# Strided attention on one core: jumps taken out, waits declared as implied, buffers fixed, key and value preparation merged, zeros written by VectorE

## The chip, the cores and the metric

The kernel runs on one core of a Trainium2 chip. The time is device time in microseconds (us), the median of several runs. In the profile the engines are PE (TensorE, with its weight loads as PEld), DVE (VectorE), ACT (ScalarE), POOL (GpSimd) and SP (SyncE, which here only issues transfers).

## The reference

Attention over 8 x 12 = 96 heads, 1024 queries of 64 numbers each, in which every query attends to the same 16 keys: positions 0, 64, 128 and so on.

```python
batch, heads, seq, dim = (8, 12, 1024, 64)      # stride = 64, all float32
scale = 1.0 / np.sqrt(dim)
for i in range(seq):
    attend_positions = np.arange(0, seq, stride)
    q = Q[:, :, i:i + 1, :]
    k = K[:, :, attend_positions, :]
    v = V[:, :, attend_positions, :]
    scores = np.einsum('bhqd,bhkd->bhqk', q, k) * scale
    weights = np.exp(scores - np.max(scores, axis=-1, keepdims=True))
    weights = weights / (np.sum(weights, axis=-1, keepdims=True) + 1e-10)
    result[:, :, i, :] = np.einsum('bhqk,bhkd->bhqd', weights, v)[:, :, 0, :]
```

Q is read whole and the result is written whole, 25.2 MB each; of K and V only one row in 64 is read, 0.4 MB each.

## The kernel before, in words

The 96 heads are worked on in 24 groups of four. The order of the work is written out by hand: every engine executes its instructions in the order in which the program names them, and semaphores hold an instruction until what it needs is there.

**Transfers.** SP issues all of them, in one queue: K, Q of group 0, V, Q of groups 1 to 9 (`load`, ten buffers `qn`), and then in turn the result of group g (`store`, eight buffers `out_sb`) and Q of group g+10, up to group 23; the last ten are stores alone. That makes 50 transfers; 48 of them move 1 MB. Loads of groups 0 and 1 move pieces of 8 KB, the later loads pieces of 32 KB, stores pieces of 8 KB, K and V rows of 256 bytes. Each transfer also waits for the one issued eight before it, whose semaphore it uses again. All 1 MB transfers are written with the helper at L34, so L34 is both loads and stores. K is L100, V is L103.

**Preparation.** POOL makes an identity matrix and from it `perm_v` (L128), a matrix that replicates rows of V. VectorE and POOL write zeros into `k_t` (L132 for the first 8 groups, L134 for the other 16) and VectorE into `w_all` (L133). VectorE works out a selector `s_sel` from an iota (L136, L137), and from it the ones beside V (L138) and `mask` (L139). `key_rows` casts a third of K (L149, ScalarE) and transposes it (L150, VectorE); `keys` spreads it over `k_t` in copies of 32 partitions (L160). `value_rows` replicates half of V by two matmuls (L171) and evacuates each (L175). The first third of K and the first half of V come ahead of the loop, the rest inside it, at groups 1 to 7 and 4.

**A group.** `cast` turns Q into bfloat16, one half on POOL (L191), one on ScalarE (L192); `transpose` turns it on VectorE (L196); `scores` is four matmuls (L203) and two exponentials (L214, ScalarE); `values` multiplies V by the mask (L182, POOL); `outputs` is eight matmuls in three portions (L228), the reciprocal of the sums (L236, VectorE) and the product: two portions on VectorE (L238), the third copied by ScalarE (L240) and scaled by POOL (L241). Work ahead is staggered: while group g is put out, scores are made for g+1, transpose and values for g+2, casts for g+3.

**Alignment.** L87 and L102 call `addr_align(128, max_nops=0)` on VectorE, POOL and SP. It lets the following instruction stand at a multiple of 128 in the engine's stream and reaches it by a jump.

Buffers `qn`, `out_sb` and `qb` come from pools that hand them out in turn, and the framework derives every wait from who read and wrote a buffer before.

Of the kernel before, what the change touches and what calls it, by code (L numbers as in the profile page):

```python
# [9 lines left out]

FP32 = mybir.dt.float32
BF16 = mybir.dt.bfloat16
I16 = mybir.dt.int16
I32 = mybir.dt.int32
AF = mybir.ActivationFunctionType
ALU = mybir.AluOpType
# [8 lines left out]
def _copy(nc, out: bass.AP, in_: bass.AP):  # L25

    sides = [
        mybir.BassSymbolicTensorAccessPattern(
            ap=side.ap, dtype=side.dtype, bass_ap=side,
            is_dma=True, for_custom_bir_dma=True,  # L30
        )
        for side in (in_, out)
    ]
    return nc.sync.add_instruction(  # L34
        mybir.InstDMACopy(
            name=nc.get_next_instruction_name(), engine=mybir.EngineType.SP,
            ins=sides[:1], outs=sides[1:], queue="qSPDynamicHW",
            mode="Copy",
        )
    )  # L40
# [9 lines left out]
def kernel(  # L50
# [22 lines left out]
    OBUFS = 8  # L73

    const = ctx.enter_context(tc.tile_pool(name="const", bufs=1))
    qn_pool = ctx.enter_context(tc.tile_pool(name="qn", bufs=QBUFS))
    out_pool = ctx.enter_context(tc.tile_pool(name="outsb", bufs=OBUFS))
    qb_pool = ctx.enter_context(tc.tile_pool(name="qb", bufs=2))
# [14 lines left out]
    qn = {}  # L93

    def load(g):
        qn[g] = qn_pool.tile([P, 32 * D], FP32, name="qn", tag="qn")
        n = P if g < 2 else 32
        _copy(nc, qn[g], _ap_with(Q, [[HG * SD // n, n], [1, HG * SD // n]], g * HG * SD))

    nc.sync.dma_start(k_raw, _ap_with(K, kv_src))  # L100
    load(0)
    nc.sync.addr_align(128, max_nops=0)  # L102
    nc.sync.dma_start(v_raw, _ap_with(V, kv_src))  # L103
    for g in range(1, QBUFS):
        load(g)


    identity = const.tile([P, P], BF16, name="identity")
    ahead4 = const.tile([P, 4], I16, name="ahead4")
    slot4 = const.tile([P, 4], I16, name="slot4")  # L110
# [8 lines left out]
    nc.gpsimd.iota(ahead4, pattern=[[-16, 4]], base=64, channel_multiplier=1)  # L119
# [6 lines left out]
    for c in range(2):  # L126
        for a in range(2):
# [4 lines left out]
    nc.vector.memset(k_t[:, 0:8], 0.0)  # L132
    nc.vector.memset(w_all, 0.0)  # L133
    nc.gpsimd.memset(k_t[:, 8:NG], 0.0)  # L134

    nc.vector.tensor_single_scalar(out=slot4, in_=ahead4, scalar=48, op=ALU.bitwise_and)  # L136
# [7 lines left out]
    v_rep = const.tile([P, NC, 2, D], BF16, name="v_rep")  # L144


    def key_rows(m):
        part = slice(4 * m, 4 * m + 4)
# [7 lines left out]
    def keys(m, c):  # L156
        for s in range(4):
            src, dst, col = 32 * (2 * c + s % 2), 32 * (2 * (s % 2) + s // 2), NK + 32 * s
            op = nc.vector.tensor_copy if m == 0 and s >= 2 else nc.scalar.copy
            op(  # L160
                k_t[dst : dst + 32, 8 * m + c : 8 * m + 8 : 2, :, col : col + NK],
                k_r[src : src + 32, 4 * m : 4 * m + 4].rearrange(
                    "p n (a k f) -> p a n f k", a=2, f=2
                )[:, s // 2],
            )


    def value_rows(n):
        for c in range(2):
            vp = psum_sc.tile([P, NC // 2, D], FP32, name="vp", tag="sc")  # L170
            nc.tensor.matmul(  # L171
                vp, lhsT=perm_v[:, c].rearrange("p a b e k -> p (a b e k)"),
                rhs=v_bf[:, 6 * n : 6 * n + 6], start=True, stop=True,
            )
            nc.vector.tensor_copy(out=v_rep[:, 6 * n : 6 * n + 6, c], in_=vp)  # L175

    qb, qt, wt, vb, rec, out_sb = {}, {}, {}, {}, {}, {}


    def values(g):  # L180
        vb[g] = v_bufs[g % 3]
        nc.gpsimd.tensor_tensor(  # L182
            out=vb[g][:, 0 : 4 * D].rearrange("p (s d) -> p s d", s=4), in0=mask,
            in1=v_rep[:, g // 2, g % 2].unsqueeze(1).to_broadcast([P, 4, D]),
            op=ALU.mult,
        )

    def cast(g):
        qb[g] = qb_pool.tile([P, 32 * D], BF16, name="qb", tag="qb")
        half = 16 * D  # L190
        nc.gpsimd.tensor_copy(out=qb[g][:, 0:half], in_=qn[g][:, 0:half])  # L191
        nc.scalar.copy(qb[g][:, half:], qn[g][:, half:])  # L192

    def transpose(g):
        qt[g] = qt_pool.tile([P, 32 * D], BF16, name="qt", tag="qt")
        nc.vector.transpose(qt[g].bitcast(I32), qb[g].bitcast(I32))  # L196

    def scores(g):
        sc = psum_sc.tile([P, 512], FP32, name="sc", tag="sc")
        q = qt[g]  # L200
        for e in range(2):
            for f in range(2):
                nc.tensor.matmul(  # L203
                    sc, lhsT=k_t[:, g, f, NK * (1 - e) : NK * (1 - e) + P],
                    rhs=_ap_with(
                        q, [q.ap[0], [D, 8], [16 * D, 2], [2, 32]],
                        extra_offset=8 * D * e + f,
                    ),
                    start=e + f == 0, stop=e + f == 2,
                )  # L210
        w = wt[g] = w_bufs[g % 3]
        for a in range(2):
            wa = w[64 * a : 64 * a + 64]
            nc.scalar.activation(  # L214
                out=_ap_with(wa, [wa.ap[0], [P, 8], [1, 2], [2, 32]], extra_offset=64 * a),
                in_=sc[64 * a : 64 * a + 64].rearrange("p (t x q) -> p t x q", t=8, x=2),
                func=AF.Exp, bias=0.0, scale=scale,
            )


    def outputs(g, c):
        if c == 0:
            out_sb[g] = out_pool.tile([P, 4, 8, D], FP32, name="out_sb", tag="out_sb")
# [12 lines left out]
        nc.vector.reciprocal(r, ps[:, 0:n, 4 * D : 4 * D + 4])  # L236
        if c < 2:
            nc.vector.tensor_tensor(out=to, in0=o, in1=by, op=ALU.mult)  # L238
        else:
            nc.scalar.copy(to, o)  # L240
            nc.gpsimd.tensor_tensor(out=to, in0=to, in1=by, op=ALU.mult)  # L241

    def store(g):
        o = out_sb[g]
        _copy(
            nc,
            _ap_with(out, [[16 * D, P], [2 * SD, 2], [1, 16 * D]], g * HG * SD),
            _ap_with(o, [o.ap[0], [1, 1], [1, 32 * D]]),
        )

    key_rows(0)
    keys(0, 0)
    cast(0)
    transpose(0)
    keys(0, 1)
# [19 lines left out]
    for g in range(NG):  # L275
        if g > 0:
            ahead(g)
        for c in range(3):
            outputs(g, c)
        if g == 0:  # L280
            ahead(g)
        if g in (1, 5):
            key_rows(g // 4 + 1)
        if g in (2, 3, 6, 7):
            keys(g // 4 + 1, g % 4 - 2)
        if g == 4:
            value_rows(1)
        store(g)
        if g + QBUFS < NG:
            load(g + QBUFS)  # L290
# [33 lines left out]
```

## Time and profile before

| | |
|---|---|
| time, median of 3 runs | 128.98 us (128.76 to 129.75) |
| the profiled execution, its own time | 128.94 us |
| its span, first to last instruction | 127.2 us |
| busy: VectorE, ScalarE, POOL, TensorE | 88.4, 86.0, 79.5, 64.3 us |
| moved by DMA | 51.20 MB, mean 403 GB/s |
| a store, from issue to landing (least, median, most) | 10.1, 13.5, 19.6 us |

A page of the profile gives busy time by engine, the span in 40 slices of 3.2 us (busy share in tenths; for DMA the mean of 16 engines, and GB/s), the DMA queues, the chain of waits followed back from the last instruction, and groups of instructions by line. The trace behind it also answers for any stretch of time (windows), lists instructions in order of time, and keeps a record of every DMA packet and of every landing, that is, of each of the 16 semaphore steps with which a transfer ends. In a timeline line the columns are start, duration, engine, line, operation, out<-in and, in brackets, idle time before and what ended it; SPq is SP's queue of issues. Times in the text are from the start of the span.

### The profile page before, as it was taken

The numbers are of one execution on the slowest core, as the hardware profiler recorded it, in microseconds if no ns is written. First come the engines' busy times: TensorE is split into PE (matmuls) and PEld (weight loads), VectorE is DVE, ScalarE is ACT, GpSimd is POOL, SyncE is SP. The second block draws the span as 40 slices with busy tenths as digits, with TensorE's granted clock in tenths as the row PEclk, the third lists the DMA queues.
The fourth block names the chain that finished last, engine by engine and source line by source line (L and its number), as shares of the span: only waits on it lengthen the run. The fifth ranks groups of instructions, "written<-read, shape, count | busy, mean of one in ns | idle before, by whom it ended". The sixth has DMA issues, their size and how long they took to land.

```text
span 127.2 us, 1226 instructions
## 1 busy us (share of the span) xinstructions
PE 64.3 (51%) x292; PEld 30.2 (24%) x292; DVE 88.4 (69%) x162; ACT 86.0 (68%) x120; POOL 79.5 (62%) x84
## 2 busy tenths in 40 slices
PE   0006548196757619662787636666463797430000
PEld 0002223042323304330333313233232343110000
DVE  4956592769698786877887889797988876760000
ACT  4151917957999986999958997979798765620000
POOL 6941818645855994595867896969889673454000
PEclk9999999755699995999657999999999558975555
DMA  2999999989998998998999989989999999999980
GB/s 67 374 329 474 464 412 423 464 381 394 451 451 381 459 464 343 487 433 376 500 387 405 497 353 438 461 374 451 428 402 451 397 433 420 425 433 417 428 350 26
DMA packets 7911, 51.20 MB, mean 403 GB/s; under 512 B 3872, under 2 KB 3872, under 8 KB 3872
## 3 DMA queue, kind: packets, MB, share of 16 engines
q1 hardware_dynamic: 7904, 51.12, 96.5%
q8 instruction: 2, 0.03, 0.1%
q14 instruction: 5, 0.04, 0.1%
HBM read 25.95 MB, written 25.17 MB: 402 GB/s over the span
## 4 chain that ended last, share of the span: by engine, by line
POOL 35%; issue 32%; DMA 15%; DVE 4%; PE 2%; ACT 1%; POOLq 1%; SPq 0%; DVEq 0%
POOL qb L191 14%; POOL out_sb L241 12%; POOL v_all L182 9%; DMA out_dram<-out_sb 9%; DMA qn<-in_Q_dram 5%; PE sc L203 1%; POOLq L319 1%; DVE out_sb L238 1%; DVE qt L196 1%; DVE v_rep L175 1%; ACT qb L192 1%; PE vp L171 1%; ACT out_sb L240 1%; DVE rec L236 0%; SPq L100 0%
## 5 line engine op out<-in xcount | busy, mean ns | idle before, releaser
L228 PE MATMUL o_ps<-v_all,w_all 128*128 128x260 bf16 x192 | 38.4, 320 | 37.1 <-DVE out_sb L238 32.8
L241 POOL TENSOR_TENSOR out_sb<-out_sb,rec 128x768 f32<-128x768 f32 x24 | 35.3, 1471 | 29.8 <-ACT out_sb L240 29.8
L238 DVE TENSOR_TENSOR out_sb<-o_ps,rec 128x768 f32<-128x768 f32 (+1 forms) x48 | 39.6, 825 | 1.7
L214 ACT ACTIVATE w_all<-sc 64x512 bf16<-64x512 f32 x48 | 35.2, 734 | 5.5 <-PE sc L203 4.9
L203 PE MATMUL sc<-qt,k_t 128*128 128x512 bf16 x96 | 32.0, 466 | 10.7 <-DVE qt L196 10.7
L196 DVE STREAM_TRANSPOSE qt<-qb 128x1024 int32<-128x1024 int32 x24 | 29.6, 1232 | 10.8 <-ACT qb L192 5.7
L228 PEld LDWEIGHTS <-w_all 128*128 128x128 bf16 x192 | 18.9, 109 | 60.3 <-DVE out_sb L238 41.2
L240 ACT COPY out_sb<-o_ps 128x768 f32<-128x768 f32 x24 | 19.2, 798 | 16.1 <-DVE rec L236 15.8
L191 POOL CAST qb<-qn 128x1024 bf16<-128x1024 f32 x24 | 24.9, 1036 | 4.7 <-DMA qn<-in_Q_dram 4.7
L192 ACT CAST qb<-qn 128x1024 bf16<-128x1024 f32 x24 | 25.0, 1045 | 0.7
L236 DVE RECIPROCAL rec<-o_ps 128x12 f32<-128x12 f32 (+1 forms) x72 | 15.1, 210 | 6.3 <-PE o_ps L228 5.8
L182 POOL TENSOR_TENSOR v_all<-mask,v_rep 128x256 bf16<-128x256 bf16 x24 | 16.0, 668 | 0.6 <-DVE v_rep L175 0.6
L203 PEld LDWEIGHTS <-k_t 128*128 128x128 bf16 x96 | 10.8, 113 | 21.6 <-ACT k_t L160 8.1
L160 ACT COPY k_t<-k_r 32x128 bf16<-32x128 bf16 x20 | 5.9, 295 | 2.1 <-DVE k_r L150 1.9
L134 POOL MEMSET k_t<- 128x4608 bf16 x1 | 3.9, 3938 | 0.0
L175 DVE CAST v_rep<-vp 128x384 bf16<-128x384 f32 x4 | 2.2, 542 | 1.9 <-PE vp L171 1.8
L149 ACT CAST k_bf<-k_raw 128x256 bf16<-128x256 f32 x3 | 1.2, 406 | 3.2 <-DMA k_raw<-in_K_dram 3.2
L150 DVE STREAM_TRANSPOSE k_r<-k_bf 128x128 int32<-128x128 int32 x3 | 0.9, 310 | 2.3 <-ACT k_bf L149 2.3
L136 DVE TENSOR_SCALAR slot<-ahead 128x4 int16<-128x4 int16 x1 | 2.5, 2482 | 0.0
L171 PE MATMUL vp<-v_bf,perm_v 128*128 128x384 bf16 x4 | 1.6, 412 | 1.1 <-DVE v_rep L175 0.6
L132 DVE MEMSET k_t<- 128x1152 uint32 x1 | 1.0, 1018 | 1.6 <-PEq L305 1.6
L149 ACT ACT_TABLE_LOAD x1 | 1.3, 1283 | 0.7 <-PEq L305 0.7
(15 smaller groups left out, 5.7 us busy)
## 6 DMA issues: line engine op xcount, KB each, us to landing
qn<-in_Q_dram SPq DMA_DIRECT2D x24, 1024.0 KB, 14.7
out_dram<-out_sb SPq DMA_DIRECT2D x24, 1024.0 KB, 13.5
k_raw<-in_K_dram SPq DMA_DIRECT2D x1, 384.0 KB, 4.5
v_raw<-in_V_dram SPq DMA_DIRECT2D x1, 384.0 KB, 7.4
```

The lines of the kernel that those rows point to most:

```text
L160: op(k_t[dst : dst + 32, 8 * m + c : 8 * m + 8 : 2, :, col : col + NK], k_r[src : src + 32, 4 * m : 4 * m + 4].rearrange("p n (a k f) -> p ...
L182: nc.gpsimd.tensor_tensor(out=vb[g][:, 0 : 4 * D].rearrange("p (s d) -> p s d", s=4), in0=mask, in1=v_rep[:, g // 2, g % 2].unsqueeze(1).t ...
L191: nc.gpsimd.tensor_copy(out=qb[g][:, 0:half], in_=qn[g][:, 0:half])
L192: nc.scalar.copy(qb[g][:, half:], qn[g][:, half:])
L196: nc.vector.transpose(qt[g].bitcast(I32), qb[g].bitcast(I32))
L203: nc.tensor.matmul(sc, lhsT=k_t[:, g, f, NK * (1 - e) : NK * (1 - e) + P], rhs=_ap_with(q, [q.ap[0], [D, 8], [16 * D, 2], [2, 32]], extra_ ...
L214: nc.scalar.activation(out=_ap_with(wa, [wa.ap[0], [P, 8], [1, 2], [2, 32]], extra_offset=64 * a), in_=sc[64 * a : 64 * a + 64].rearrange( ...
L228: nc.tensor.matmul(ps[:, i, 0 : 4 * D + 4], lhsT=wt[g][:, i0 + i], rhs=vb[g], start=True, stop=True,)
L236: nc.vector.reciprocal(r, ps[:, 0:n, 4 * D : 4 * D + 4])
L238: nc.vector.tensor_tensor(out=to, in0=o, in1=by, op=ALU.mult)
L240: nc.scalar.copy(to, o)
L241: nc.gpsimd.tensor_tensor(out=to, in0=to, in1=by, op=ALU.mult)
```

## The change

- The jumps (L87, L102) are gone.
- `qn`, `qb` and `out_sb` are fixed buffers, indexed by group. For pairs of instructions between which another wait already guarantees the order, `implied` tells the framework to make no wait. `transpose(g)` gets a wait for store g−10, so that VectorE has waited for an output buffer before ScalarE and POOL use it.
- All of `k_t` is zeroed by VectorE. The selector comes from the identity by a reduction; its two copies move from VectorE to POOL.
- K is prepared in two parts (4 and 8 of 12) in place of three; copies that VectorE made for the first part are POOL's. The cast of V moves from VectorE to POOL.
- `value_rows` puts both matmuls into one slot of `o_ps` and evacuates them with one instruction.

```diff
-    for engine in (nc.vector, nc.gpsimd):
-        engine.addr_align(128, max_nops=0)
...
+    qn_bufs = [const.tile([P, 32 * D], FP32, name=f"qn{i}") for i in range(QBUFS)]
+    qb_bufs = [const.tile([P, 32 * D], BF16, name=f"qb{i}") for i in range(2)]
+    out_bufs = [const.tile([P, 4, 8, D], FP32, name=f"out_sb{i}") for i in range(OBUFS)]
...
+    def implied(ins, earlier, why):
+        tc.declare_no_dep(ins.ins, earlier.ins, reason=why)
...
     def load(g):
-        qn[g] = qn_pool.tile([P, 32 * D], FP32, name="qn", tag="qn")
+        qn[g] = qn_bufs[g % QBUFS]
...
+        if g >= QBUFS:
+            for earlier in (loaded[g - QBUFS], *cast_by[g - QBUFS]):
+                implied(loaded[g], earlier, "the store before it has waited for both casts")
...
     load(0)
-    nc.sync.addr_align(128, max_nops=0)
     nc.sync.dma_start(v_raw, _ap_with(V, kv_src))
...
-    nc.vector.memset(k_t[:, 0:8], 0.0)
+    nc.vector.memset(k_t, 0.0)
     nc.vector.memset(w_all, 0.0)
-    nc.gpsimd.memset(k_t[:, 8:NG], 0.0)
-
-    nc.vector.tensor_single_scalar(out=slot4, in_=ahead4, scalar=48, op=ALU.bitwise_and)
-    nc.vector.tensor_single_scalar(out=s_sel, in_=slot4, scalar=0, op=ALU.is_equal)
-    nc.vector.tensor_copy(out=v_all[:, :, 4 * D :], in_=s_sel.unsqueeze(1).to_broadcast([P, 3, 4]))
-    nc.vector.tensor_copy(out=mask, in_=s_sel.unsqueeze(2).to_broadcast([P, 4, D]))
+
+    nc.vector.tensor_reduce(
+        out=s_sel, in_=identity.rearrange("p (h s k) -> p s h k", h=2, s=4),
+        op=ALU.max, axis=mybir.AxisListType.XY,
+    )
+    nc.gpsimd.tensor_copy(out=v_all[:, :, 4 * D :], in_=s_sel.unsqueeze(1).to_broadcast([P, 3, 4]))
+    nc.gpsimd.tensor_copy(out=mask, in_=s_sel.unsqueeze(2).to_broadcast([P, 4, D]))
...
+    def keys(part, c, s):
+        src, dst, col = 32 * (2 * c + s % 2), 32 * (2 * (s % 2) + s // 2), NK + 32 * s
+        op = nc.gpsimd.tensor_copy if part is first and s >= 2 else nc.scalar.copy
...
     def value_rows(n):
+        vp = psum_o.tile([P, 3, 512], FP32, name="o_ps", tag="o")
+        rows = vp[:, 0:2, 0 : NC // 2 * D].rearrange("p c (n d) -> p c n d", d=D)
         for c in range(2):
-            vp = psum_sc.tile([P, NC // 2, D], FP32, name="vp", tag="sc")
...
-            nc.vector.tensor_copy(out=v_rep[:, 6 * n : 6 * n + 6, c], in_=vp)
+        nc.vector.tensor_copy(
+            out=v_rep[:, 6 * n : 6 * n + 6].rearrange("p n c d -> p c n d"), in_=rows
+        )
...
     def transpose(g):
         qt[g] = qt_pool.tile([P, 32 * D], BF16, name="qt", tag="qt")
-        nc.vector.transpose(qt[g].bitcast(I32), qb[g].bitcast(I32))
+        turned = nc.vector.transpose(qt[g].bitcast(I32), qb[g].bitcast(I32))
+        if g - 2 >= OBUFS:
+            tc.add_manual_dep(
+                turned.ins, stored[g - 2 - OBUFS].ins.name,
+                mybir.DependencyInfo(mybir.DependencyClass.Sync, mybir.DependencyReason.ANTI),
+                reason="frees the output buffer that VectorE fills next",
+            )
...
-            nc.scalar.copy(to, o)
-            nc.gpsimd.tensor_tensor(out=to, in0=to, in1=by, op=ALU.mult)
+            copied = nc.scalar.copy(to, o)
+            scaled[g] = nc.gpsimd.tensor_tensor(out=to, in0=to, in1=by, op=ALU.mult)
+            for past in range(g - OBUFS, -1, -OBUFS):
+                for earlier in (stored[past], scaled[past]):
+                    implied(copied, earlier, "VectorE has waited for the store")
+                implied(scaled[g], stored[past], "VectorE has waited for the store")
...
-    nc.vector.tensor_copy(out=v_bf, in_=v_raw)
+    nc.gpsimd.tensor_copy(out=v_bf, in_=v_raw)
     value_rows(0)
...
-        if g in (1, 5):
-            key_rows(g // 4 + 1)
-        if g in (2, 3, 6, 7):
-            keys(g // 4 + 1, g % 4 - 2)
+        if g == 1:
+            key_rows(rest)
+        if 2 <= g < 6:
+            for i in range(2 * g - 4, 2 * g - 2):
+                keys(rest, i // 4, i % 4)
         if g == 4:
             value_rows(1)
```

The casts, the exponentials and the masked values get `implied` declarations of the same kind, against the same instruction two or three groups earlier. Lines named in the prediction are those of the kernel before, but L205, which is `transpose` in the changed kernel.

More of the change, by code (lines that the diff above doesn't have):

```diff
@@ L12 @@
 BF16 = mybir.dt.bfloat16
-I16 = mybir.dt.int16
 I32 = mybir.dt.int32
@@ L144, with key_rows @@
     v_rep = const.tile([P, NC, 2, D], BF16, name="v_rep")
-    def key_rows(m):
-        part = slice(4 * m, 4 * m + 4)
+    def key_rows(part):
         nc.scalar.copy(k_bf[:, part], k_raw[:, part])
@@ L153, in key_rows @@
         )
[L156 to L165, printed above, removed]
+    def keys(part, c, s):
+        src, dst, col = 32 * (2 * c + s % 2), 32 * (2 * (s % 2) + s // 2), NK + 32 * s
+        op = nc.gpsimd.tensor_copy if part is first and s >= 2 else nc.scalar.copy
+        op(
+            k_t[dst : dst + 32, 2 * part.start + c : 2 * part.stop : 2, :, col : col + NK],
+            k_r[src : src + 32, part].rearrange(
+                "p n (a k f) -> p a n f k", a=2, f=2
+            )[:, s // 2],
+        )
     def value_rows(n):
+        vp = psum_o.tile([P, 3, 512], FP32, name="o_ps", tag="o")
+        rows = vp[:, 0:2, 0 : NC // 2 * D].rearrange("p c (n d) -> p c n d", d=D)
         for c in range(2):
-            vp = psum_sc.tile([P, NC // 2, D], FP32, name="vp", tag="sc")
             nc.tensor.matmul(
-                vp, lhsT=perm_v[:, c].rearrange("p a b e k -> p (a b e k)"),
+                rows[:, c], lhsT=perm_v[:, c].rearrange("p a b e k -> p (a b e k)"),
                 rhs=v_bf[:, 6 * n : 6 * n + 6], start=True, stop=True,
             )
-            nc.vector.tensor_copy(out=v_rep[:, 6 * n : 6 * n + 6, c], in_=vp)
+        nc.vector.tensor_copy(
+            out=v_rep[:, 6 * n : 6 * n + 6].rearrange("p n c d -> p c n d"), in_=rows
+        )
     qb, qt, wt, vb, rec, out_sb = {}, {}, {}, {}, {}, {}
@@ L181, in values @@
         vb[g] = v_bufs[g % 3]
-        nc.gpsimd.tensor_tensor(
+        masked[g] = nc.gpsimd.tensor_tensor(
             out=vb[g][:, 0 : 4 * D].rearrange("p (s d) -> p s d", s=4), in0=mask,
@@ L186, in values @@
         )
+        if g >= 3:
+            implied(masked[g], masked[g - 3], "the matmuls between them")
     def cast(g):
-        qb[g] = qb_pool.tile([P, 32 * D], BF16, name="qb", tag="qb")
+        qb[g] = qb_bufs[g % 2]
         half = 16 * D
-        nc.gpsimd.tensor_copy(out=qb[g][:, 0:half], in_=qn[g][:, 0:half])
-        nc.scalar.copy(qb[g][:, half:], qn[g][:, half:])
+        cast_by[g] = (
+            nc.gpsimd.tensor_copy(out=qb[g][:, 0:half], in_=qn[g][:, 0:half]),
+            nc.scalar.copy(qb[g][:, half:], qn[g][:, half:]),
+        )
+        if g >= 2:
+            for h in range(2):
+                for e in range(2):
+                    implied(cast_by[g][h], cast_by[g - 2][e], "the transpose between them")
     def transpose(g):
         qt[g] = qt_pool.tile([P, 32 * D], BF16, name="qt", tag="qt")
-        nc.vector.transpose(qt[g].bitcast(I32), qb[g].bitcast(I32))
+        turned = nc.vector.transpose(qt[g].bitcast(I32), qb[g].bitcast(I32))
[4 more added lines that the diff above has]
+                reason="frees the output buffer that VectorE fills next",
+            )
     def scores(g):
@@ L211, in scores @@
         w = wt[g] = w_bufs[g % 3]
+        raised[g] = []
         for a in range(2):
             wa = w[64 * a : 64 * a + 64]
-            nc.scalar.activation(
+            raised[g].append(nc.scalar.activation(
                 out=_ap_with(wa, [wa.ap[0], [P, 8], [1, 2], [2, 32]], extra_offset=64 * a),
@@ L217, in scores @@
                 func=AF.Exp, bias=0.0, scale=scale,
-            )
+            ))
+            for earlier in raised.get(g - 3, ()):
+                implied(raised[g][a], earlier, "the matmuls between them")
     def outputs(g, c):
         if c == 0:
-            out_sb[g] = out_pool.tile([P, 4, 8, D], FP32, name="out_sb", tag="out_sb")
+            out_sb[g] = out_bufs[g % OBUFS]
             rec[g] = rec_pool.tile([P, 8, 4], FP32, name="rec", tag="rec")
@@ L239, in outputs @@
         else:
-            nc.scalar.copy(to, o)
-            nc.gpsimd.tensor_tensor(out=to, in0=to, in1=by, op=ALU.mult)
+            copied = nc.scalar.copy(to, o)
[4 more added lines that the diff above has]
+                implied(scaled[g], stored[past], "VectorE has waited for the store")
     def store(g):
         o = out_sb[g]
-        _copy(
+        stored[g] = _copy(
             nc,
@@ L249, in store @@
         )
-    key_rows(0)
-    keys(0, 0)
+    first, rest = slice(0, 4), slice(4, NC)
+    key_rows(first)
+    for s in range(4):
+        keys(first, 0, s)
     cast(0)
     transpose(0)
-    keys(0, 1)
+    for s in range(4):
+        keys(first, 1, s)
     scores(0)
     cast(1)
-    nc.vector.tensor_copy(out=v_bf, in_=v_raw)
+    nc.gpsimd.tensor_copy(out=v_bf, in_=v_raw)
     value_rows(0)
```

11 lines of the change are left out of this document (3 added, 8 removed).

## The prediction, on record before the changed kernel ran

> **What bounds the kernel now.** I read the slices of the page first (part 2), then its queues (part 3), then the table of windows, and only then the engines.
>
> ```profile
> DMA  2999999989998998998999989989999999999980
> GB/s 67 374 329 474 464 412 423 464 381 394 451 451 381 459 464 343 487 433 376 500 387 405 497 353 438 461 374 451 428 402 451 397 433 420 425 433 417 428 350 26
> q1 hardware_dynamic: 7904, 51.12, 96.5%
> q8 instruction: 2, 0.03, 0.1%
> q14 instruction: 5, 0.04, 0.1%
> ```
>
> No computing engine is over 69% busy, but the one data queue keeps the 16 DMA engines busy for 96.5% of the span. The digits fall only in the first slice and the last two. The windows say the same with less jitter (after the PE, PEld, DVE, ACT and POOL columns come granted clock, DMA share, GB/s):
>
> ```profile
> 12.00:28.00 16.00, 9.64 (x34) 3.98 (x33) 9.40 (x17) 10.54 (x14) 8.76 (x10) 0.87 1.00 428
> 52.00:80.00 28.00, 17.55 (x89) 8.81 (x90) 23.45 (x44) 24.69 (x34) 21.18 (x22) 0.88 1.00 425
> 114.00:122.00 8.00, 0.00 (x0) 0.00 (x0) 0.00 (x0) 0.24 (x1) 1.47 (x1) 0.50 1.02 427
> ```
>
> In the last window almost nothing computes any more and the rate is what it was at 52 us: the queue has a full backlog from start to finish. So the chain of waits, which gives POOL 35% of the span, misleads: it follows computation back, while what ends last is the queue.
>
> From the landing records (16 per transfer, one for each DMA engine) I take the time apart. The first packet starts at 2.07 us; the mean landing of the 50th transfer is 124.42, so 51.12 MB took 122.35 us; its slowest engine lands 1.73 us after that mean; the span closes 1.02 us later, at 127.17; 1.74 us lie outside the span. The sum is 128.94, the profiled execution's own time, 0.04 under the median of the runs shown (128.98).
>
> **How much cover computation has.** SP issues the transfers in program order:
>
> ```profile
> 2.47 0.39 SPq L103 DMA_DIRECT2D v_raw<-in_V_dram  x1
> 2.91 9.84 SPq L34 DMA_DIRECT2D qn<-in_Q_dram  x9
> 21.14 0.63 SPq L34 DMA_DIRECT2D out_dram<-out_sb  x1
> 28.77 0.59 SPq L34 DMA_DIRECT2D out_dram<-out_sb  x1
> ...
> 112.93 3.43 SPq L34 DMA_DIRECT2D out_dram<-out_sb  x2
> ```
>
> A transfer needs 1.34 us from issue to first packet (0.73 to 2.07, the first one). The queue stays full if each is issued that long before its predecessor lands. The twelfth transfer lands at 30.86 (mean), so the first store may be issued up to 29.5 and is issued at 21.14: 8.4 us of cover. The second store (28.77) follows load 10, which lands at 35.76: 5.6 us. The last is issued at 115.8, and its predecessor lands at 121.98: 4.9 us. These are the two thinnest places. At the end cover does not depend on how fast computation runs before: load 23 lands complete at 101.24, POOL casts it at 102.00, and the last store follows 13.8 us after that cast, while ten stores (2.46 us each) are still to be moved after load 23.
>
> **The change, part by part.**
>
> *Jumps gone (L87, L102).* SP's jump lies between the issue of Q0, which ends at 1.95, and of V at 2.47: about 0.5 us. VectorE starts at 1.61 where ScalarE starts at 0.73: up to 0.9 us. POOL waits 0.83 us before L119. V is issued 0.5 us sooner, but the records show all 16 engines on K and Q0 until V's first packets at 6.4: worth 0. K's issue, at 0.73, stands before SP's jump and stays.
>
> *Shorter streams.* The built programs fall from 211 to 186 instructions on VectorE, 167 to 121 on ScalarE, 140 to 109 on POOL, 102 to 91 on SP; TensorE keeps 615. Most are separate semaphore waits: 42 to 5 on ScalarE, 45 to 10 on POOL. One takes 21 ns (median on VectorE's queue) or 17 ns (SP's), so 0.8, 0.7, 0.3 and 0.2 us on ScalarE, POOL, VectorE and SP, all under the queue. Fewer instructions also mean fewer fetches. In the packet records q14 moves 8 KB at 2.04, 3.18, 6.88, 48.85 and 81.97 us, 0.31 to 0.62 us each, and q8 16 KB at 48.58 and 91.35, 1.05 us each. A fetch holds one of 16 engines: 7 together take 4.0 us, 0.25 us of the mean. The two on q8 fall where TensorE has gone through some 190 and 430 instructions, so I take them as TensorE's and unchanged. If the five go, the mean gains 1.92/16 = 0.1 us. The slowest engine may gain more. Its lag is already 1.05 us at the second transfer, while the next slowest has 0.72, and it grows to 1.73. A fetch of 0.62 us at 2.04 lies just there. If it was on that engine and goes, the lag falls by 0.33, to the next engine's. Bounds: the whole 1.73 gone, or, with streams that now start unaligned, four fetches of 0.31 more on the slowest engine, +1.2. I take −0.3, by the row it comes from.
>
> [...]
>
> *Zeros on VectorE alone.* L132 takes 1.018 us for 1152 words, so 3456 words take 3.05; w_all keeps 1.34. POOL loses the 3.94 us of L134:
>
> ```profile
> 1.61 1.02 DVE L132 MEMSET k_t<- 128x1152 uint32 x1 [1.61 <-PEq L305]
> 2.67 3.94 POOL L134 MEMSET k_t<- 128x4608 bf16 x1
> 4.15 2.48 DVE L136 TENSOR_SCALAR slot<-ahead 128x4 int16<-128x4 int16 x1
> ```
>
> The odd row is the third: 2.48 us for four elements, ending at 6.63 when POOL's memset ends at 6.61; the next row like it (L137) takes 0.17. That stall goes. The new reduction lies between 0.17 (L137) and 0.56 (L258, 768 elements); 0.3. VectorE starts between 0.73 and 1.61 and is through at 5.4 to 6.6; k_bf is ready at 5.61, so the key transpose starts at 5.7 to 6.6, not 7.15. Worth 0: the first scores still wait for Q0, which lands at 8.2.
>
> *Keys, selector and V cast on POOL.* Two small copies of the selector and four of 32x128 join POOL: each above 0.22 (VectorE) and below 0.67 (L182, 256 elements), I take 0.4. They fit before 8.25 and, the last two, between 9.3 and the first scores at 10.67. What gets later is V. POOL takes its cast behind that of Q1, which starts at 12.31 and takes 1.04; the cast is 768/1024 of that, 0.78, bounds 0.56 (L258) and 1.04. Ready at 14.1, two matmuls (0.5 each) to 15.1, one evacuation in place of two (0.54 to 1.08) to 16.2, transpose(1) behind it to 17.5, then the first values (0.67) are in. The first reciprocal comes at about 18, not 16.39: 1.6 us later, 2.1 by the upper bounds. The first two stores move to about 22.7 and 30.4; their covers of 8.4 and 5.6 us swallow it, and past that each us of delay is a us at the end.
>
> *Merged keys and values later.* On ScalarE 16 copies of 0.295 become 8 between 0.295 and 0.59: 0 to 2.4 us saved. VectorE's two key transposes of 0.31 become one of 0.31 to 0.62. value_rows now takes a slot of o_ps: TensorE waits for one evacuation more (0.96), once at group 0 and once at group 4. Covered.
>
> *The new wait (L205).* From group 10 on, transpose(g) waits for store(g−10). Behind it in VectorE's queue stand the reciprocals and products of group g−2, which in the kernel before waited for that same store about 2.4 us later. It is thinnest at g = 23: the trace has that transpose at 103.07 and store 13 complete at 98.83. It holds by 4.2 us; if computation gains more than that, it only gives the surplus back. Worth 0.
>
> **Sum:** 128.94 − 0.1 − 0.3 = 128.5, all of it in how the fetches lie on the DMA engines; everything else is under the queue. With half of the −0.1 kept (two q14 fetches may stay), 128.6.
>
> [...]
>
> **The rivals.** *Forecast: the queue decides, 128.6* (87%). In it lies the case that the fetches do not change at all, that shorter streams fetch as often: 128.9.
>
> *Faster, 127.1* (7%): the lag of the slowest engine comes from the fetches as a whole. For it: the landing spread widens in steps near 48, 82 and 91 us, where fetches lie. Against: 1.05 of the 1.73 is there from the second transfer on and the lag creeps between steps; TensorE's two fetches stay. It needs 1.3 of 1.73 us.
>
> *Slower, 131* (6%): the V path through POOL lets the queue run dry before the second store. It decides once that store is issued after 34.4 (35.76 − 1.34). A delay of 8 us, to 36.8, would cost 2.4 us: 128.6 + 2.4 = 131.0. For it: three POOL instructions now stand between Q1's landing and the first values. Against: 1.6 to 2.1 us worked out; even a V cast as long as the 3.94 us memset makes 4.8.
>
> **From these to the numbers.** The runs before spread from 128.76 to 129.75, so about 1% (1.3 us) is what a measurement of this kernel can tell from no change. Range 127.9 to 129.7: below, 0.7 us more of the lag; above, the four extra fetches on the slowest engine (128.6 + 1.2 = 129.8), nearly whole. Faster 0.07, within 1% 0.87, slower 0.06.
>
> **What would show it.** Right: q1 still 51.12 MB at 96 to 97%, 425 to 428 GB/s in the same windows, first store at 22 to 24 us, last store issued well before 120, fewer than five q14 pieces, lag 1.3 to 1.7 us. Busy time of ScalarE and POOL may fall by several us with no effect. Wrong: a DMA digit under 8 between slices 3 and 37, a store issued after its predecessor's landing, or a lag that changed by over 1 us.

## The result and the profile after

The changed kernel takes 129.58 us (median, 129.29 to 129.81) beside 128.96 us of the kernel before, measured together: ratio 1.0037, 95% interval 1.0023 to 1.0050, so 0.30 to 0.64 us slower. The profiled execution took 129.29 us, of which 127.2 us are its span; the kernel before had 128.94. The profile after is of the fastest of the 22 executions, 0.29 us under their median, so it shows 0.35 us of the loss where the medians show 0.62. The prediction, 128.6 us, was 0.3% under the kernel before. The time lies in the range given and within 1%, but on the other side of no change.

The page of the changed kernel, slices of its part 2 and queues of its part 3:

```profile
DMA  2999999898998989999999989999999899999991
GB/s 65 360 320 492 423 402 454 371 474 340 505 407 369 513 348 417 461 379 438 461 384 443 477 363 469 430 387 492 402 387 484 363 420 430 425 420 430 425 410 59
q1 hardware_dynamic: 7904, 51.12, 97.0%
q8 instruction: 2, 0.03, 0.1%
q14 instruction: 4, 0.03, 0.1%
```

The queue still moves the same 51.12 MB in the same 7904 packets and still fills the span. No digit of the DMA line between slices 3 and 37 is under 8. So the queue never ran dry, and yet the kernel is slower; that points to the transfers themselves. The table of windows says where (stretch and length, then PE, PEld, DVE, ACT, POOL busy, granted clock, DMA share, GB/s):

```profile
12.00:28.00 16.00, 8.71 (x30) 3.58 (x29) 8.80 (x14) 9.91 (x12) 8.77 (x10) 0.93 0.99 416
52.00:80.00 28.00, 18.43 (x94) 9.27 (x95) 23.66 (x45) 23.96 (x30) 22.97 (x23) 0.88 1.01 428
114.00:122.00 8.00, 0.00 (x0) 0.00 (x0) 0.00 (x0) 0.00 (x0) 0.94 (x1) 0.50 1.01 425
```

In the middle and at the end the rate is that of before (425 and 427 there). In the first window, in which only loads move, it is 416 in place of 428 GB/s at a DMA share of 0.99: of these three stretches, this one alone lost, 2.8%.

The landing records, taken apart in the way of the prediction (us; an interval is that between mean landings of successive transfers):

| | before | after |
|---|---|---|
| loads Q1 to Q9, one interval | 2.427 | 2.485 |
| 12th transfer (Q9), mean landing | 30.62 | 31.27 |
| transfers 13 to 40, one interval | 2.458 | 2.453 |
| last ten stores, one interval | 2.461 | 2.464 |
| 50th transfer, mean landing | 124.18 | 124.88 |
| its slowest engine, after that | 1.73 | 1.40 |
| from that landing to the end of the measured time | 3.03 | 3.02 |
| sum: the profiled execution | 128.94 | 129.29 |

The prediction and the recorded expectations count landings and packets from a zero that lies 0.24 us ahead of the span's start, which is the zero of the timeline and of this table. Their first packet at 2.07 us is at 1.83, as the profile's own window shows, which has data moving before 2.00 us:

```profile
0.00:2.00 2.00, 0.00 (x0) 0.00 (x0) 0.39 (x1) 1.27 (x1) 0.79 (x8) 1.00 0.04 10
```

Their 30.86 is 30.62 here, and their 2.79 us from the last landing to the end is 3.03. Intervals, lags and differences between kernels are the same by either zero.

**Two terms moved, and they have opposite signs.** The lag of the slowest engine is 0.33 us less in this execution, the size forecast. The back-to-back loads became 0.058 us longer each. Nine intervals (V to Q9) make 0.52 us, V itself lands 0.12 us later (8.90 for 8.78), and the 0.65 us that the queue is behind at the 12th transfer is 0.70 at the 50th. The delay is never caught up.

The steps of the change that the prediction priced stand in the timeline of the changed kernel:

```profile
1.52 2.94 DVE L131 MEMSET k_t<- 128x3456 uint32 x1 [1.52 <-PEq L331]
2.00 0.58 SPq L105 DMA_DIRECT2D v_raw<-in_V_dram  x1
5.99 0.23 DVE L134 TENSOR_REDUCE s_sel<-identity 128x4 bf16<-128x128 bf16 x1
6.13 0.29 DVE L149 STREAM_TRANSPOSE k_r<-k_bf 128x128 int32<-128x128 int32 x1
13.00 0.82 POOL L283 CAST v_bf<-v_raw 128x768 bf16<-128x768 f32 x1
14.71 0.96 DVE L174 CAST v_rep<-o_ps 128x768 bf16<-128x768 f32 x1 [4.54 <-PE o_ps L170]
17.33 0.23 DVE L254 RECIPROCAL rec<-o_ps 128x12 f32<-128x12 f32 x1 [0.51 <-PE o_ps L246]
22.12 0.63 SPq L33 DMA_DIRECT2D out_dram<-out_sb  x1
```

V is issued at 2.00 and not 2.47, the jump's half microsecond; V's cast on POOL is ready at 13.82, the first reciprocal runs at 17.33, and the first store is issued at 22.12, 9.2 us before the 12th transfer lands at 31.27. So a queue that waits for computation is not the cause of the loss.

### The profile page after: what moved, and what is told of

Read it like the earlier page. It is cut to its first block, busy times and chain, and to the rows that moved or that the text cites. A ratio compares the mean times of both kernels' runs of the same rounds, so it can differ in the third digit from the quotient of the medians.

```text
span 127.2 us, 1113 instructions
## 1 busy us (share of the span) xinstructions
PE 62.8 (49%) x292; PEld 29.6 (23%) x292; DVE 85.3 (67%) x151; ACT 84.6 (66%) x111; POOL 78.0 (61%) x89
## 3 DMA queue, kind: packets, MB, share of 16 engines
q1 hardware_dynamic: 7904, 51.12, 97.0%
## 4 chain that ended last, share of the span: by engine, by line
DVE 30%; POOL 18%; PE 15%; ACT 14%; DMA 7%; issue 4%; SPq 1%; POOLq 1%; DVEq 0%
DVE out_sb L256 15%; DVE qt L205 9%; POOL out_sb L259 8%; DMA qn<-in_Q_dram 7%; PE sc L218 7%; PE o_ps L246 6%; ACT out_sb L258 6%; POOL qb L195 5%; DVE rec L254 5%; POOL v_all L183 3%; ACT w_all L230 3%; ACT qb L196 2%; PE o_ps L170 1%; POOLq L345 1%; ACT k_t L158 1%
## 5 line engine op out<-in xcount | busy, mean ns | idle before, releaser
L246 PE MATMUL o_ps<-v_all,w_all 128*128 128x260 bf16 x192 | 37.0, 309 | 37.2 <-DVE out_sb L256 31.3
L205 DVE STREAM_TRANSPOSE qt<-qb 128x1024 int32<-128x1024 int32 x24 | 29.5, 1231 | 12.2 <-POOL qb L195 7.0
L174 DVE CAST v_rep<-o_ps 128x768 bf16<-128x768 f32 x2 | 1.9, 958 | 5.3 <-PE o_ps L170 5.3
L158 ACT COPY k_t<-k_r 32x256 bf16<-32x256 bf16 (+1 forms) x12 | 4.4, 366 | 1.1 <-DVE k_r L149 0.9
L131 DVE MEMSET k_t<- 128x3456 uint32 x1 | 2.9, 2938 | 1.5 <-PEq L331 1.5
L148 ACT CAST k_bf<-k_raw 128x256 bf16<-128x256 f32 (+1 forms) x2 | 1.0, 512 | 3.1 <-DMA k_raw<-in_K_dram 3.1
L170 PE MATMUL o_ps<-v_bf,perm_v 128*128 128x384 bf16 x4 | 1.6, 507 | 2.1 <-POOL v_bf L283 1.8
L149 DVE STREAM_TRANSPOSE k_r<-k_bf 128x128 int32<-128x128 int32 (+1 forms) x2 | 0.7, 370 | 1.4 <-ACT k_bf L148 1.4
L132 DVE MEMSET w_all<- 128x1536 uint32 x1 | 1.3, 1338 | 0.3 <-issue 0.3
```

The source lines that it names most:

```text
L158: op(k_t[dst : dst + 32, 2 * part.start + c : 2 * part.stop : 2, :, col : col + NK], k_r[src : src + 32, part].rearrange("p n (a k f) -> p ...
L205: turned = nc.vector.transpose(qt[g].bitcast(I32), qb[g].bitcast(I32))
L246: nc.tensor.matmul(ps[:, i, 0 : 4 * D + 4], lhsT=wt[g][:, i0 + i], rhs=vb[g], start=True, stop=True,)
```

## The experiments

All ten kernels were compared with the kernel before on the same chip. Terms are those of the table above; a table of all of them stands at the end.

**What was suspected.** In the built programs the pools of the kernel before put `qn` at byte 53248 of each partition and further buffers at multiples of 4096. In the changed kernel the fixed buffers stand among the constants, right behind K and V and without a gap: the first `qn` begins at byte 22656, which is 88 x 256 + 128, and every `qn` and `out_sb` buffer begins 128 bytes past a multiple of 256. *Theory:* the start address of the buffers that loads write makes the loads slower. *Rivals:* the jumps and the fetches of instructions (the pieces on q8 and q14, whose kind the page gives as instruction; three of 8 KB at 1.80, 2.94 and 6.64 us in the kernel before), which lie among the same loads, set their rate; or what the engines do at the start does.

### Buffers of the changed kernel moved by 128 bytes

```diff
+    const.tile([P, 128], mybir.dt.uint8, name="pad")
     qn_bufs = [const.tile([P, 32 * D], FP32, name=f"qn{i}") for i in range(QBUFS)]
```

> The changed kernel with 128 unused bytes ahead of the ten Q buffers, so that every Q, cast and output buffer starts at a multiple of 256 bytes within its partition (they start 128 bytes past one in the changed kernel, at multiples of 4096 in the kernel before). Nothing else is touched. Theory (the start address of the buffers that the loads write sets the rate of the loads): nine loads Q1 to Q9 land 2.43 us apart, as before the change, not 2.49; the mean landing of the last transfer falls back by 0.5 to 0.7 us, the lag of the slowest engine stays at about 1.4, time 128.6 to 129.0, ratio to the kernel before 0.997 to 1.000. Rival one (where the instruction fetches fall, now that the jumps are gone): still 2.49 and 129.6, ratio 1.004. Rival two (the order of the computation at the start, V cast late on POOL): still 2.49 and 129.6.

Measured: 128.52 us, ratio 0.9971 (0.9951 to 0.9990). Loads are 2.428 us apart, the 12th transfer lands at 30.58. The windows of this kernel:

```profile
12.00:28.00 16.00, 9.61 (x35) 4.09 (x34) 8.71 (x14) 10.35 (x14) 8.73 (x11) 0.97 1.01 434
52.00:80.00 28.00, 16.85 (x93) 8.48 (x91) 24.59 (x46) 24.21 (x31) 23.19 (x23) 0.97 1.01 427
```

434 in place of 416 GB/s in the first window, no difference in the second. An unused strip of 128 bytes per partition turns the change from slower to faster: 1.0037 to 0.9971 is 0.66%, 0.85 us. The first `qn` now starts at 22784 = 89 x 256, which is no multiple of 512: here a multiple of 256 was enough.

### The same shift put into the kernel before

```diff
     v_rep = const.tile([P, NC, 2, D], BF16, name="v_rep")
+    const.tile([P, 128], mybir.dt.uint8, name="pad")
```

Here the strip moves what comes after the constants, `qn` and `out_sb` with the rest. Jumps, waits and instructions are those of before.

> The kernel before with 128 unused bytes at the end of its constants, which moves all Q, output and cast buffers from multiples of 4096 to 128 bytes past them. Theory of the start address: the nine loads land 2.49 us apart in place of 2.43; time up by 0.5 to 0.7 us, ratio 1.004 to 1.006. Both rivals (fetches, order of the computation): 2.43 and no change, ratio 0.999 to 1.001.

Measured: 129.74 us, ratio 1.0062 (1.0041 to 1.0083). Loads are 2.484 us apart, the lag stays at 1.73 us. The windows:

```profile
12.00:28.00 16.00, 10.53 (x36) 4.40 (x35) 9.32 (x17) 10.88 (x14) 8.77 (x10) 0.94 0.99 416
52.00:80.00 28.00, 16.43 (x82) 7.83 (x81) 22.25 (x43) 25.33 (x34) 21.84 (x23) 0.88 1.02 431
```

The same 416 GB/s, without anything else of the change. The start address is thereby shown from both sides.

### The jumps alone taken out of the kernel before

```diff
-    for engine in (nc.vector, nc.gpsimd):
-        engine.addr_align(128, max_nops=0)
...
-    nc.sync.addr_align(128, max_nops=0)
```

> The kernel before without its three jumps (the two calls of addr_align), nothing else. Theory of the start address: the loads stay at 2.43 us apart; only the fetches at the start go, so the lag of the slowest engine at the second transfer falls from 1.05 to about 0.5 to 0.7 and the time by 0.3 us, ratio 0.996 to 0.999. Rival one (fetches set the rate of the loads): 2.49 us apart, 0.5 us more, ratio 1.004. Rival two (order of the computation): no change.

Measured: 128.44 us, ratio 0.9957 (0.9935 to 0.9978). Loads are 2.428 us apart, and the first window has the 428 GB/s of the kernel before:

```profile
12.00:28.00 16.00, 9.94 (x35) 4.02 (x33) 9.96 (x17) 11.09 (x14) 9.06 (x10) 0.89 1.00 428
```

Jumps and the fetches at the start do not set the rate, and the rival falls. The time is just under the 0.996 to 0.999 forecast. The lag fell to 1.44 us, and, not looked for, the way from the last landing to the end fell from 3.03 to 2.65 us. The mean landings did not move: 30.58 for 30.62 at the 12th transfer, 124.23 for 124.18 at the 50th. The interval overlaps that of the changed kernel with aligned buffers (128.52): beyond the jumps, the shorter streams, the declared waits and the merged preparation bring nothing that these runs can tell apart.

### Only the loads' buffers aligned, and only the stores'

```diff
+    const.tile([P, 128], mybir.dt.uint8, name="pad")
     qn_bufs = [const.tile([P, 32 * D], FP32, name=f"qn{i}") for i in range(QBUFS)]
     qb_bufs = [const.tile([P, 32 * D], BF16, name=f"qb{i}") for i in range(2)]
+    const.tile([P, 128], mybir.dt.uint8, name="pad2")
     out_bufs = [const.tile([P, 4, 8, D], FP32, name=f"out_sb{i}") for i in range(OBUFS)]
```

With both strips `qn` is aligned and `out_sb` 128 bytes off:

> The changed kernel with its Q buffers moved to a multiple of 256 bytes and its output buffers left 128 bytes past one. If the writes of the loads into SBUF carry the whole cost: loads Q1 to Q9 land 2.43 us apart, the last ten transfers (stores alone) 2.46 as everywhere, time as with everything aligned, 128.5, ratio 0.996 to 0.999. If the reads of the stores carry it: 2.49 stays, 129.5.

With the second strip alone it is the other way round:

> The reverse: output buffers at a multiple of 256 bytes, Q buffers left 128 bytes past one. If the loads carry the cost: Q1 to Q9 land 2.49 us apart, last ten stores 2.46, time as the changed kernel, 129.5, ratio 1.003 to 1.006. If the stores carry it: 128.5.

Measured: loads' buffers alone aligned, 128.53 us, ratio 0.9975 (0.9964 to 0.9987); stores' alone, 129.65 us, ratio 1.0061 (1.0037 to 1.0085). The first windows, of the one and of the other:

```profile
12.00:28.00 16.00, 9.19 (x32) 3.71 (x31) 8.71 (x14) 10.02 (x13) 8.78 (x10) 0.97 1.01 434
```

```profile
12.00:28.00 16.00, 9.27 (x34) 3.98 (x34) 8.71 (x14) 10.19 (x13) 8.72 (x11) 0.98 1.00 422
```

The intervals of the loads are plainer than the windows, 2.428 and 2.484 us. The writes of the loads carry the whole effect. The last ten stores are 2.465 us apart in both kernels, whether they read from a multiple of 256 or from 128 past it.

### 64 bytes off in place of 128

```diff
+    const.tile([P, 192], mybir.dt.uint8, name="pad")
     qn_bufs = [const.tile([P, 32 * D], FP32, name=f"qn{i}") for i in range(QBUFS)]
```

> The changed kernel with Q, cast and output buffers 64 bytes past a multiple of 256 in place of 128. [...] If the cost is one more cut per piece: loads land 2.49 us apart as at 128 bytes, ratio 1.003 to 1.005. If it is by the bytes past the boundary, half of it: 2.456, ratio 1.000 to 1.002. If only multiples of 64 count, none: 2.43.

Measured: 129.34 us, ratio 1.0049 (1.0028 to 1.0070), loads 2.485 us apart. The loss at 64 bytes is that at 128 (2.485 us in both kernels), so between these two it does not go by the number of bytes. Of the three cases the numbers are those of the first; that a piece is cut once more is not shown by any record. In the packet records a 32 KB packet of the early loads takes 1218 ns with an aligned start (the kernel before) and 1243 ns (both means) with one 64 or 128 bytes past.

### K and V aligned as well

`k_raw` and `v_raw` begin 128 bytes past a multiple of 256 in both kernels. With the strip ahead of them everything after is aligned.

```diff
+    const.tile([P, 128], mybir.dt.uint8, name="pad")
     k_raw = const.tile([P, NC, D], FP32, name="k_raw")
```

> The changed kernel with the 128 unused bytes ahead of the K buffer, so that K and V too (rows of 256 bytes, 128 bytes past a multiple of 256 in both kernels so far) start at a multiple of 256, along with all other buffers. If each row of K and V is cut in two by its start and that costs time: a packet of 256 bytes falls from 18 ns to 11 to 15 ns, V takes 1.1 to 1.4 us between landings in place of 1.72, K lands 0.3 to 0.6 sooner, and the time is 0.5 to 1.2 us below the version that aligns Q and outputs alone (128.52): 127.3 to 128.0, ratio 0.988 to 0.993. If small pieces are bound by their number alone: 18 ns, 128.5, ratio 0.997.

Measured: 128.40 us, ratio 0.9959 (0.9944 to 0.9974), beside 128.52 and 0.9971 without it; the intervals overlap. The forecast was a miss. A 256-byte packet still takes 18 ns, and K lands no sooner (4.46 for 4.48). V does land sooner, 1.37 us after Q0 and not 1.72, but the loads behind it are then 2.457 us apart, with a few pieces of up to 1772 ns, and the 12th transfer lands at 30.58 as without it. Why these loads give the gain back is open.

### Jumps late in place of early

In the kernel before, POOL has exactly 130 instructions after its start jump, so a multiple of 128 falls just ahead of its last two. There, in its closing, POOL's last drain starts at 126.53 us and the next instruction only at 126.97, 0.44 us later; without jumps this gap is 0.08 us. A sixth fetch of 8 KB on q14 lies at 127.65, after the span. The hypothesis: crossing such a multiple while nothing else is left to do costs some 0.4 us at the end. In the changed kernel the gap at POOL is gone, but the way to the end is as long, 0.89 us inside the span and 2.13 outside (before: 1.25 and 1.77), so another crossing could lie there. The test takes the changed kernel with all buffers aligned and puts the alignment at group 20, from where 16 instructions (POOL), 33 (VectorE) and 17 (SP) are left in the trace:

```diff
+        if g == 20:
+            for engine in (nc.vector, nc.gpsimd, nc.sync):
+                engine.addr_align(128, max_nops=0)
```

> The version of the changed kernel with Q and output buffers at a multiple of 256 bytes, with three jumps put in late: at group 20 VectorE, POOL and SP each jump to a multiple of 128 in their streams. From the last landing to the end of the measured time it took 2.78 us in the kernel before (1.02 of it inside the span, with a gap of 0.44 us in POOL's closing) and 2.78 in the changed one (0.70 inside, 2.1 outside the span), and 2.41 only in the kernel before without jumps. Theory (one engine's stream crosses a multiple of 128 in the closing, where nothing hides it): with the crossing put at group 20, 0.69 inside and 1.75 outside, 2.41 in all, time 128.52 - 0.37 = 128.15, ratio 0.994. Rival (the 0.36 us outside the span belong to something else in the changed kernel): 2.78 stays, 128.5, ratio 0.997.

Measured: 128.20 us, ratio 0.9946 (0.9929 to 0.9964), and 2.66 us from the last landing to the end. The term fell by the amount forecast, from 3.04 us. Since three engines were moved at once, which of them made the 0.36 us outside the span in the changed kernel stays open, and that a crossing is the cause fits the counts but is not shown by itself.

### The start jumps put back

```diff
+    for engine in (nc.vector, nc.gpsimd):
+        engine.addr_align(128, max_nops=0)
...
+    const.tile([P, 128], mybir.dt.uint8, name="pad")
...
+    nc.sync.addr_align(128, max_nops=0)
```

> The same version with the three jumps of the kernel before put back at its start. If the jumps bring the fetches of 8 KB at 2 to 7 us, and these the lag of the slowest engine: fetches near 2.0, 3.2 and 6.9 us return, the lag at the second transfer goes from 0.35 to about 1.05, the last landing comes 0.2 to 0.5 us later, time 128.7 to 129.0, ratio 0.998 to 1.001. If the lag is chance: no change, 128.5, ratio 0.997.

Measured: 128.53 us, ratio 0.9971 (0.9953 to 0.9989): the forecast was a miss, the time is that without jumps. Two terms cancel. SP's pause is back:

```profile
1.23 0.72 SPq L33 DMA_DIRECT2D qn<-in_Q_dram  x1
2.49 0.39 SPq L110 DMA_DIRECT2D v_raw<-in_V_dram  x1
```

With it Q0 lands 0.38 us later than without the jumps (7.39 for 7.01) and the 12th transfer 0.30 later (30.88 for 30.58), at an unchanged interval of 2.427 us; at the 50th 0.16 us are left. The lag at the second transfer is 0.64, not 1.05 us. And the way from the last landing to the end is 2.65 us, which fits the hypothesis: POOL has 100 instructions after its jump here, and no multiple of 128 falls near the end. Beside the kernel with late jumps, whose closing is as short, this one takes 0.33 us more (128.53 for 128.20; the intervals just overlap). So the jumps at the start seem to cost some 0.3 us, but by which term is open: the three fetches of 8 KB, at 1.75, 3.03 and 6.53 us, lie among the late landings here, while in the kernel before the jumps moved the 12th landing by 0.04 us only and the lag of the slowest engine by 0.29.

### All of it together

Everything aligned, no jumps at the start, and the late alignment.

```diff
+    const.tile([P, 128], mybir.dt.uint8, name="pad")
     k_raw = const.tile([P, NC, D], FP32, name="k_raw")
...
+        if g == 20:
+            for engine in (nc.vector, nc.gpsimd, nc.sync):
+                engine.addr_align(128, max_nops=0)
```

> All at once: K, V, Q and output buffers at a multiple of 256 bytes, no jumps at the start, three jumps at group 20. By the sum of the terms: 128.4 (with K and V aligned) - 0.37 = 128.0, ratio 0.993, below the kernel before, the changed one and every version so far. If the late jumps do nothing: 128.4, ratio 0.996.

Measured: 128.03 us, ratio 0.9924 (0.9907 to 0.9940), faster than both kernels: 0.76% under the kernel before, and by the two ratios 1.1% under the changed one. From its page:

```profile
span 126.2 us, 1116 instructions
...
q1 hardware_dynamic: 7904, 51.12, 97.1%
q8 instruction: 2, 0.03, 0.1%
q14 instruction: 6, 0.05, 0.1%
```

It moves the same bytes and has more fetches on q14 than the kernel before (6 for 5); they lie after 48 us. So the number of fetches alone does not decide. Against the kernel with late jumps alone (128.20) the intervals overlap.

### The terms side by side

```
kernel                      loads   Q9     50th    slowest  last to  profiled  median   ratio
                            apart  lands   lands   engine     end       us       us
before                      2.427  30.62  124.18    1.73     3.03     128.94   128.96   1
after                       2.485  31.27  124.88    1.40     3.02     129.29   129.58   1.0037
after, all buffers aligned  2.428  30.58  124.26    1.23     3.04     128.53   128.52   0.9971
before, shifted             2.484  31.20  124.70    1.73     3.01     129.44   129.74   1.0062
before, no jumps            2.428  30.58  124.23    1.44     2.65     128.33   128.44   0.9957
after, qn aligned           2.428  30.60  124.21    1.28     3.02     128.51   128.53   0.9975
after, out_sb aligned       2.484  31.32  124.93    1.90     3.04     129.86   129.65   1.0061
after, 64 bytes off         2.485  31.13  124.82    1.48     3.03     129.34   129.34   1.0049
K and V aligned as well     2.457  30.58  124.18    0.98     3.07     128.22   128.40   0.9959
aligned, late jumps         2.428  30.55  124.24    1.11     2.66     128.01   128.20   0.9946
aligned, start jumps back   2.427  30.88  124.42    1.22     2.65     128.29   128.53   0.9971
K and V too, late jumps     2.456  30.48  124.16    1.17     2.70     128.03   128.03   0.9924
```

"All buffers" means `qn`, `qb` and `out_sb`. The columns before the median are of one profiled execution each.

## Why the prediction was wrong, point by point

**The step that failed is the Sum:** "all of it in how the fetches lie on the DMA engines; everything else is under the queue". The bound was right, and for that reason a change in the transfers themselves had to be a term of the sum. The fixed buffers were weighed by the waits they save or add, not by where they lie. They lie 128 bytes past a multiple of 256, and the loads that write them take 2.485 us and not 2.427 as long as loads follow loads. +0.65 us by the 12th transfer was missing. With it the Sum would have read 128.94 + 0.65 − 0.4 = 129.2, beside the 129.29 of the profiled execution.

The start addresses stand in the built programs and were to be had before the run. That 128 bytes matter, no trace of before shows. The 2.4% of an interval, and a loss as large at 64 bytes as at 128, come from the runs. By them it is the written side of the loads that shows the effect (2.485 us for 2.427), and the read side of the stores shows none (2.465 us in both cases). How the start address makes the loads longer was not shown.

**The shorter streams and the fetches: near in size, and partly by luck.** The forecast was −0.1 and −0.3 us. With the buffers aligned the change gives 0.37 us (ratio 0.9971). In the profiled execution of the changed kernel the lag is 1.40 us, 0.33 less; the early fetches are gone, and q14 has four pieces and not five. That fewer instructions mean fewer fetches holds in one pair of runs and not in the other: without jumps q14 has five pieces in the kernel before and four in the changed one, with the jumps at the start five in both; with jumps at group 20 it has six. That one fetch at the start sat on the slowest engine is not shown, and the landing records tell another story. Before, the lag is 1.05 us at the second transfer and still 1.10 at the 20th. After, it falls further than forecast, to 0.55 at the second and 0.33 at the 19th, and then rises to 1.26 at the 20th in one step, at 49 to 51 us, where a fetch of 16 KB (49.05 us, 1.13 us long) and two of 8 KB lie. Every kernel without jumps at the start shows such a step, of 0.8 to 1.3 us between the 18th and the 20th transfer, beside its first 16 KB fetch. That the fetch makes it is likely, not shown, since the landings name no engine. So −0.33 is the sum of a larger gain and a new loss, and without start jumps the final lag lies anywhere between 0.98 and 1.90 us in single executions. What putting the jumps back moved is told above: 0.30 us at the 12th landing, where the prediction had priced the mean at 0.1.

**Arithmetic of the prediction.** With its early zero, 1.34 us from issue to first packet is 1.10 by the timeline; the landings shift by as much, so its covers stand. Its last two terms are 1.25 and 1.77 us, not 1.02 and 1.74; as written, its first sum comes to 128.91 and not 128.94. Neither slip changes the forecast.

**A term that was not in the sum:** the time from the last landing to the end. It was taken as fixed, and it is 3.01 to 3.07 us in some kernels and 2.65 to 2.70 in others. The change left its length alone (3.03 and 3.02), so it did not spoil the forecast, but some 0.37 us could have been had there.

**Right, step by step.** The queue bounds the kernel: 97% and the same rate at 52 to 80 and 114 to 122 us. Zeros by VectorE were priced at 3.05 us and took 2.94; the 2.48 us stall is gone; the key transpose starts at 6.13 (5.7 to 6.6). V's cast is ready at 13.82 (14.1), its evacuation ends at 15.67 (16.2), the first reciprocal starts at 17.33 (18). The first two stores follow, from the timeline:

```profile
22.12 0.63 SPq L33 DMA_DIRECT2D out_dram<-out_sb  x1
29.75 0.59 SPq L33 DMA_DIRECT2D out_dram<-out_sb  x1
```

22.7 and 30.4 were forecast. The second needed to be out by 34.4, so the rival at 131 us, V's path through POOL, was never near its point of decision. POOL's small copies were put at 0.4 us each and took 0.19 (beside V), 0.40 (mask) and 0.31 (keys). The new wait on store g−10 held nothing up.

**The rivals.** The faster one, 127.1 by a lag that vanishes, did not come: no kernel here has a lag under 0.98 us. Its cause, fetches, and its objection, that the two on q8 stay (they start at 48.34 and 91.11 us before, at 49.05 and 90.37 after), both fit the step at 49 us; that these two are TensorE's was the author's inference from their times. The slower one named one mechanism, computation that leaves the queue empty; the loss came by another, a queue that is full and slower. The criterion "425 to 428 GB/s in the same windows" caught it at once: 416 in the first.

## What to carry to other kernels

Where one queue bounds a kernel, take an edit that moves a buffer as an edit of the transfers (a shift of 128 bytes and nothing else made the kernel before 0.6% slower, ratio 1.0062): compare the start addresses in the built programs, and try the buffers that loads write at a multiple of 256 bytes (here 2.427 us for a load of 1 MB in place of 2.485). When a change is meant to thin out instructions, take the time apart at the landings (rate of the loads alone, rate beside stores, slowest engine, closing), for two terms of opposite sign can hide in 0.4%. Take the profile of an execution near the median, or say how far off it is. In these runs jumps at group 20 gave the short closing without early fetches; where streams cross a multiple of 128 instructions is worth a look when the closing seems long (3.03 us in the kernel before, 2.65 without its jumps), though that the crossing is the cause was not shown.

## What the runs showed of the hardware

- A load whose buffer rows begin 64 or 128 bytes past a multiple of 256 took 2.484 to 2.485 us in place of 2.427 to 2.428 per MB when loads followed each other (2.456 to 2.457 in the two kernels in which K and V are aligned as well). Where they alternate with stores there is no difference (2.447 to 2.461 us in all the kernels). Why not is open. Stores that read from 128 bytes past such a multiple lose nothing (2.465 us each, as from a multiple).
- In the closing the kernels fall into two groups, 3.01 to 3.07 and 2.65 to 2.70 us after the last landing. In the kernel before the difference lies inside the span, at POOL (1.25 us for 0.88 without jumps); in the changed kernel it lies outside it (2.13 for 1.77 us with late jumps).
- With the jumps at the start came three early fetches of 8 KB (at 1.80, 2.94 and 6.64 us in the kernel before, at 1.75, 3.03 and 6.53 in the changed kernel with aligned buffers); the changed kernel has none before 48.98 us. In the changed kernel with aligned buffers the 12th transfer then landed 0.30 us later (30.88 for 30.58), though the loads keep their 2.427 us; in the kernel before, 0.04 us later (30.62 for 30.58). Why the two differ is open.
- In the kernels without jumps at the start, the lag of the slowest engine rises by 0.8 to 1.3 us in the two transfers that land at 48 to 51 us, beside a fetch of 16 KB that takes 0.95 to 1.13 us.
